# Seven-product K pairs of a two-layer trunk: another order of the products, and one more such pair in each layer's down projection

## The chip, the cores and the metric

The kernel runs on one core of one Trainium2 chip. The metric is the device time of one execution in microseconds (us). Engines are named as in the profile: PE (TensorE) does the matmuls, PEld is its weight load, DVE is VectorE, ACT is ScalarE, POOL is GpSimd, SP is SyncE, which here only starts DMAs. A row such as "L281 DVE TENSOR_TENSOR Tl<-G,Th" is an instruction that line 281 of the kernel issued on DVE and that wrote the tile Tl from the tiles G and Th.

## The reference

Two layers act on 256 tokens of width 2048. Each has a mixer (one input projection, two kinds of attention, an output projection) and a gated feed-forward part of width 5632, each between two RMS norms:

```python
D_MODEL = 2048
SEQ = 256
DEPTH = 2
D_FF = (-(-8 * D_MODEL // 3) + 255) // 256 * 256      # 5632

def swiglu(h, w_gate, w_up, w_down):
    return (jax.nn.silu(h @ w_gate) * (h @ w_up)) @ w_down

def reference(x, w_in, w_o, ..., w_gate, w_up, w_down):
    for l in range(DEPTH):
        h = rms_norm(x, pre_mix_norm[l])
        m = hybrid_mixer(h, l, w_in[l], w_o[l], ...)
        x = x + rms_norm(m, post_mix_norm[l])
        h = rms_norm(x, pre_ffn_norm[l])
        f = swiglu(h, w_gate[l], w_up[l], w_down[l])
        x = x + rms_norm(f, post_ffn_norm[l])
    return x
```

Everything is float32. Nearly all of the work is in the projections `h @ w_in`, `mix @ w_o`, `h @ w_gate`, `h @ w_up` and `... @ w_down`.

## The kernel before

**Weights.** All weights lie in memory in the order in which they are used, cut into pairs of 512 KB. A pair holds two blocks of 128 rows (K) by 512 columns. SP loads them into tiles `raw` (a ring of four). PE multiplies in a rounded float32, so each pair is split: ACT writes the high part `hi` (L307, or L279 in a mixed pair) and DVE the low part `lo` (L317, or L281). `hi` and `lo` are rings of six. A product of tokens and weights is then three matmuls with a moving block of 512 columns: high by high (L1084), high by low (L1085), low by high (L1086).

**Eight and seven.** A K pair (256 rows of K) for two column blocks and two halves of the tokens is a 2 by 2 by 2 block product: eight products, 24 matmuls. Those are `eight` in gate and up (matmuls at L1250) and `down` (L1356, L1357, L1359). For chosen K pairs the kernel uses the Strassen–Winograd form with seven products, 21 matmuls: `seven_products` (L1105), called for the input projection (L1066), the output projection (L1173), gate and up (L1257) and down (L1368). It sums into the four result banks `banks` and into four further banks, `p1`, `p6`, `p7` and `q5`, which `shared_part` (L1122) adds to the results once, after the last seven of a group of columns.

The seven products need sums of tokens and sums of weights. `token_sums` (L1088) makes the four token sums s1 to s4 on DVE (L1091 to L1094) and splits them into `sh` (ACT, L1101) and `sl` (DVE, L1102). `mixed_weights` (L263) makes the weights of five products out of two loaded pairs. The first pair is loaded into `G`. The second is loaded into `T` by SP (L257), and POOL adds a block of the first one to it with an accumulating DMA (L258). Then, in order:

- t1 and b22 are the two halves of the pair split from `T`: `hi` by ACT, `lo` by DVE at L281
- t2 is a difference inside `T` (DVE, L290, 128x512); its parts are `Th` (ACT, L279) and `Tl` (DVE, L281, 128x512)
- `G` plus t2 (DVE, L291, 128x1024) gives t3 and t4; their parts are `Th` (ACT, L279) and `Tl` (DVE, L281, 128x1024)

So t3 is the weight that is ready last but for t4, which comes out of the same operation. `Th` and `Tl` are rings of two. `G` and `T` are rings of three (`T` of four in gate).

**Stages of a layer.** The input projection runs first, then attention, then the output projection (matmuls at L569 to L571 in `unit`), whose result is normalized (`rescale`, L595 to L627, with its square root as a logarithm and an exponential on ACT, L602 and L603) and turned by PE (`transposed`, L485) with the parts read off by ACT (L488) and DVE (L493). Gate and up then run in 11 chunks of 512 columns, eight K pairs each, of which chunk 0 has two sevens, chunk 1 three, chunks 2 and 10 four, and chunks 3 to 9 five:

```python
SEVEN = (2, 4, 5, 6)
MORE_SEVEN = (2, 3, 4, 5, 6)
MORE_AT = (3, 4, 5, 6, 7, 8, 9)
MORE_ORDER = (0, 2, 1, 3, 4, 5, 6, 7)
```

Down runs in two halves of 1024 columns with 22 K pairs each. `DOWN_SEVEN` (L51) lists, for either half, the K pairs that are sevens. Before each K pair, tokens are split into `jh` (ACT, L1332) and `jl` (DVE, L1334), up to two K pairs ahead, in rings of four.

**What sets the order.** The code is written in the order of the products, with weights split four pairs ahead (`LOOKAHEAD`). A scheduler of the language then places the instructions on each engine: they run in program order on an engine in the end, but that order is the scheduler's, which can put a ready instruction ahead of an earlier one. Side chains (attention, transposes of a finished chunk) are advanced by `tick`. So the order in which `seven_products` issues its products also moves instructions of DVE and ACT.

Of the kernel before, what the change touches and what calls it, by code (L numbers as in the profile page):

```python
# [47 lines left out]
MORE_AT = (3, 4, 5, 6, 7, 8, 9)  # L48
MORE_ORDER = (0, 2, 1, 3, 4, 5, 6, 7)
FORM_AT = {(0, 1): 4, (0, 2): 6, (0, 5): 5, (1, 3): 2, (2, 4): 3}  # L50
DOWN_SEVEN = ((4, 7, 10, 12, 15, 17, 20), (3, 5, 8, 10, 13, 15, 18))  # L51

AFTER = mybir.DependencyInfo(mybir.DependencyClass.Sync, mybir.DependencyReason.DATA)

# [26 lines left out]
def weight_order():  # L81
# [3 lines left out]
    def queue_pair(name, l, kp, c):  # L85
        order.append((name, l, kp, c))
        return len(order) - 1
# [3 lines left out]
    for l in range(L):  # L91
# [20 lines left out]
        for half in range(2):  # L112
            for kp in range(FF // P // 2):
                for c in (2 * half, 2 * half + 1):
                    lay["down"][c, kp] = queue_pair("w_down", l, kp, c)
                if kp in DOWN_SEVEN[half]:
                    sevens.add(lay["down"][2 * half + 1, kp])
# [50 lines left out]
def kernel(  # L168
# [30 lines left out]
    def four_banks(odd, names):  # L199
        makers = (bank, bank, bank, last_bank) if odd else (acc_bank,) * 4  # L200
        return [make(n) for make, n in zip(makers, names)]
# [143 lines left out]
    def weights(i, ahead):  # L345
        feed(i + 1 + ahead)
        return ready[i]
# [198 lines left out]
    def tick():  # L546
        clock[0] += 1
        for e in list(running):
            if e[0] <= clock[0]:
                try:  # L550
                    n = next(e[1])
                    e[0] = clock[0] + (PACE if n is None else n)
                except StopIteration:
                    running.remove(e)
# [508 lines left out]
    def seven_in(banks, extra, sums, xT, l, cc, kp, first, last):  # L1063
        hi, lo = weights(plan[l]["in"][cc[0], kp], LOOKAHEAD)
        m = weights(plan[l]["in"][cc[1], kp], LOOKAHEAD)
        seven_products(banks, extra, sums, *pair_blocks(xT, kp), hi, lo, m, first, last)  # L1066
# [14 lines left out]
    def product(a, stat, moving, first, last):  # L1081
        sh, sl = stat
        hi, lo = moving
        nc.tensor.matmul(a, sh, hi, start=first, stop=False, skip_group_check=open_sums[0])  # L1084
        nc.tensor.matmul(a, sh, lo, start=False, stop=False, skip_group_check=open_sums[0])  # L1085
        return nc.tensor.matmul(a, sl, hi, start=False, stop=last, skip_group_check=open_sums[0])  # L1086
# [18 lines left out]
    def seven_products(banks, extra, sums, a11, a12, a22, hi, lo, m, first, last):  # L1105
        s1, s2, s3, s4 = sums
        p1, p6, p7, q5 = extra
        todo = (
            (p1, a11, (hi[:, 0, :], lo[:, 0, :]), first, last),
            (banks[0], a12, (hi[:, 1, :], lo[:, 1, :]), False, False),  # L1110
            (q5, s1, m["t1"], first, last),
            (p7, s3, m["t3"], first, last),
            (p6, s2, m["t2"], first, last),
            (banks[1], s4, m["b22"], False, False),
            (banks[2], a22, m["t4"], False, False),
        )
        for n, job in enumerate(todo):
            if n % 2 == 0:
                tick()
            newest_seven[0] = product(*job)  # L1120
# [14 lines left out]
    for l in range(L):  # L1135
# [27 lines left out]
        for kp in LATE_O:  # L1163
            i, j = (plan[l]["o"][c, kp] for c in (2, 3))
            if kp not in O_SEVEN:
                for c, i in ((2, i), (3, j)):
                    unit({t: accs[c, t] for t in range(NT)}, mix, i, kp, range(NT), kp == LATE_O[0], False)
                continue
            if kp == O_SEVEN[0]:
                extra = four_banks(False, [f"{q}_o{l}" for q in ("p1", "p6", "p7", "q5")])  # L1170
            hi, lo = weights(i, LOOKAHEAD)
            m = weights(j, LOOKAHEAD)
            seven_products(got, extra, forms[kp], *pair_blocks(mix, kp), hi, lo, m, kp == O_SEVEN[0], kp == O_SEVEN[-1])  # L1173
            if kp == O_SEVEN[-1]:
                for t in range(NT):
                    mg[t, 1] = pool.tile([P, 2, CW], F32, tag="qk", bufs=4, name=f"mg_o{l}_{t}_1")
                shared_part(extra, [mg[t, 1][:, h, :] for t in range(NT) for h in range(2)])
                for c in (2, 3):
                    nc.vector.tensor_tensor(out=accs[c, 1], in0=accs[c, 1], in1=mg[1, 1][:, c - 2, :], op=shared_sign(1, c - 2))
# [72 lines left out]
        def seven(banks, extra, c, kp, first, last):  # L1252
            hi, lo = weights(plan[l]["gate"][c, kp], LOOKAHEAD)
            m = weights(plan[l]["up"][c, kp], LOOKAHEAD)
            e, o = xT[2 * kp], xT[2 * kp + 1]
            a11, a12, a22 = (e[:, 0, 0:P], e[:, 1, 0:P]), (o[:, 0, 0:P], o[:, 1, 0:P]), (o[:, 0, P:S], o[:, 1, P:S])
            seven_products(banks, extra, forms[kp], a11, a12, a22, hi, lo, m, first, last)  # L1257

        for c in range(FF // CW):
            banks = four_banks(1 - c % 2, [f"c{q}_{l}_{c}" for q in ("11", "12", "21", "22")])  # L1260
# [62 lines left out]
        for half in range(2):  # L1323
            split, forms = {}, {}
            mine = DOWN_SEVEN[half]

# [71 lines left out]
            for t in range(NT):  # L1398
# [4 lines left out]
                for c in cc:  # L1403
                    for kp in range(nkp - tail, nkp):
# [4 lines left out]
                        for kk in range(2):  # L1409
                            sh, sl = jh[:, kk, t * P : (t + 1) * P], jl[:, kk, t * P : (t + 1) * P]  # L1410
                            last = kp == nkp - 1 and kk == 1
# [63 lines left out]
```

## Time and profile before

Three runs took 2187.52 to 2189.52 us.

| what | before |
|---|---|
| median of the runs | 2189.1 us |
| the profiled execution, its own time | 2188.99 us |
| its span, first to last instruction | 2187.3 us |
| granted clock of TensorE | 0.999 |
| busy DVE, ACT, POOL | 88%, 64%, 11% of the span |
| DMA queues of SP: bytes, share of the 16 engines | 436 MB, 57.7% |
| DMA queue of POOL | 32.6 MB, 8.9% |

The span is the profiled execution without what lies before its first and after its last instruction. Busy time of PE counts pipelined matmuls with modelled ends; a row's duration is longer than the step from one matmul to the next. Rows of a group read: line, engine, operation, output<-inputs, shapes, count, then busy us and mean ns of one, then the idle time of the engine just before them and what ended it. Rows of a timeline read: start, duration, engine, line, operation, with idle before and its releaser in brackets. Rows of waits read: who waited for whom, us in total, times, longest.

### The profile page before, as it was taken

The page shows a single profiled execution, that of the slowest core. Times are in us where ns is not written, and L with a number is a line of the kernel's source. Part 1 is how long each engine was busy: PE and PEld are TensorE (multiplying, and loading weights), DVE is VectorE, ACT ScalarE, POOL GpSimd, SP SyncE. Part 2 cuts the span into 40 slices and gives each one's busy share as a digit, 9 for nine tenths or more (in the row PEclk, how much of TensorE's full clock was granted, in tenths as well). Part 3 has the DMA queues.
Part 4 walks back from the last instruction along what each step waited for, and adds up shares of the span by engine and source line. Part 5 has one row for each costly group of instructions (what it writes and reads, how often), then busy time and mean ns, then how long its engine had stood idle before and what let it go on. Part 6 is the DMA issues. An engine that isn't in the chain of part 4 may idle for free.

```text
span 2187.3 us, 28757 instructions
## 1 busy us (share of the span) xinstructions
PE 2170.0 (99%) x9950; PEld 1782.2 (81%) x9950; DVE 1914.1 (88%) x2639; ACT 1393.4 (64%) x2083; POOL 251.1 (11%) x241
## 2 busy tenths in 40 slices
PE   9999999999999999999999999999999999999998
PEld 7888888788888888888878888887888888888886
DVE  7888658999999999989878886589999999999997
ACT  7666665766666656666665656657566666666664
POOL 2100000031221220000010000001212212200000
PEclk9999999999999999999999999999999999999999
DMA  9545554587887876767465555555878877767683
GB/s 324 194 163 174 192 189 168 184 291 234 243 261 222 234 228 228 231 216 255 146 241 174 181 176 182 193 170 184 292 226 255 249 222 231 239 216 233 207 265 101
DMA packets 140563, 470.96 MB, mean 215 GB/s; under 512 B 15984, under 2 KB 17008, under 8 KB 139904
## 3 DMA queue, kind: packets, MB, share of 16 engines
q1 hardware_dynamic: 121952, 436.03, 57.7%
q0 software_dynamic: 17888, 32.55, 8.9%
q8 instruction: 78, 1.28, 0.2%
q10 hardware_dynamic: 576, 0.54, 0.1%
q14 instruction: 69, 0.57, 0.1%
HBM read 460.67 MB, written 8.39 MB: 214 GB/s over the span
## 4 chain that ended last, share of the span: by engine, by line
PE 87%; DVE 7%; issue 2%; DMA 2%; ACT 1%; SPq 0%; DVEq 0%; ACTq 0%
PE c L1250 16%; PE in L1084 7%; PE in L1086 7%; PE in L1085 7%; PE dn L1356 4%; PE dn L1357 4%; PE dn L1359 4%; PE p L1085 2%; PE c L1086 2%; PE c L1084 2%; PE c L1085 2%; PE p L1086 2%; PE p L1084 2%; PE o L569 2%; PE o L570 2%
## 5 line engine op out<-in xcount | busy, mean ns | idle before, releaser
L317 DVE TENSOR_TENSOR lo<-raw,hi 128x1024 fp32r<-128x1024 f32 x472 | 567.8, 1221 | 99.0 <-ACT hi L307 97.9
L307 ACT ACTIVATE hi<-raw 128x1024 fp32r<-128x1024 f32 x494 | 509.8, 1055 | 144.2 <-PE c L1086 36.8
L1250 PE MATMUL c<-hi,xF 128*128 128x512 f32 x1280 | 346.0, 391 | 0.1
L1250 PEld LDWEIGHTS c<-hi,xF 128*128 128x128 f32 x1280 | 238.3, 188 | 49.1 <-DVE xF L493 0.6
L258 POOL DMA_DIRECT2D T<-in_weights_in_turn_dram x124 | 108.8, 877 | 1343.6 <-DMA T<-in_weights_in_turn_dram 764.8
L1250 PE MATMUL c<-lo,xF 128*128 128x512 f32 x640 | 198.2, 390 | 2.5 <-DVE lo L317 2.5
L1356 PE MATMUL dn<-hi,jh 128*128 128x512 f32 x432 | 168.2, 389 | 0.0
L1357 PE MATMUL dn<-lo,jh 128*128 128x512 f32 x432 | 168.1, 389 | 0.0
L307 ACT ACTIVATE hi<-G 128x1024 fp32r<-128x1024 f32 x124 | 131.1, 1057 | 52.1 <-DMA G<-in_weights_in_turn_dram 20.8
L281 DVE TENSOR_TENSOR Tl<-G,Th 128x1024 fp32r<-128x1024 f32 x124 | 151.2, 1220 | 14.5 <-ACT Th L279 14.5
L279 ACT ACTIVATE hi<-T 128x1024 fp32r<-128x1024 f32 x124 | 130.3, 1051 | 51.0 <-PE c L1086 29.8
L279 ACT ACTIVATE Th<-G 128x1024 fp32r<-128x1024 f32 x124 | 130.8, 1055 | 47.8 <-DVE G L291 47.5
L281 DVE TENSOR_TENSOR lo<-T,hi 128x1024 fp32r<-128x1024 f32 x124 | 156.5, 1262 | 2.9 <-ACT hi L279 2.4
L291 DVE TENSOR_TENSOR G<-G,T 128x1024 f32<-128x1024 f32 x124 | 151.2, 1219 | 2.1
L1250 PEld LDWEIGHTS c<-lo,xF 128*128 128x128 f32 x640 | 120.1, 188 | 28.2 <-DVE lo L317 3.0
L317 DVE TENSOR_TENSOR lo<-G,hi 128x1024 fp32r<-128x1024 f32 x106 | 129.2, 1219 | 12.2 <-ACT hi L307 12.0
L1359 PE MATMUL dn<-hi,jl 128*128 128x512 f32 x432 | 133.0, 389 | 0.0
L1084 PE MATMUL in<-hi,xT 128*128 128x512 f32 x328 | 131.4, 402 | 0.5 <-ACT hi L889 0.5
L279 ACT ACTIVATE Th<-T 128x512 fp32r<-128x512 f32 x124 | 78.2, 631 | 83.6 <-DVE T L290 82.9
L1084 PE MATMUL in<-hi,xI 128*128 128x512 f32 x328 | 131.1, 401 | 0.0
L1085 PE MATMUL in<-lo,xI 128*128 128x512 f32 x328 | 128.0, 390 | 0.3 <-DVE lo L317 0.3
L1086 PE MATMUL in<-hi,xI 128*128 128x512 f32 x328 | 127.9, 391 | 0.0
(485 smaller groups left out, 4917.7 us busy)
## 6 DMA issues: line engine op xcount, KB each, us to landing
raw<-in_weights_in_turn_dram SPq DMA_DIRECT2D x494, 512.0 KB, 4.6
T<-in_weights_in_turn_dram SPq DMA_DIRECT2D x124, 512.0 KB, 5.5
G<-in_weights_in_turn_dram SPq DMA_DIRECT2D x124, 512.0 KB, 5.6
T<-in_weights_in_turn_dram POOLq DMA_DIRECT2D x124, 256.0 KB, 5.7
GU<-in_weights_in_turn_dram SPq DMA_DIRECT2D x32, 512.0 KB, 6.2
V<-in_weights_in_turn_dram SPq DMA_DIRECT2D x8, 512.0 KB, 3.9
away_ffn<-x SPq DMA_DIRECT2D x8, 512.0 KB, 7.4
xd<-away_ffn SPq DMA_DIRECT2D x8, 512.0 KB, 9.5
```

The costliest lines, as they stand in the source:

```text
L279: nc.scalar.activation(h, w, AF.Copy)
L281: newest_rest[i] = nc.vector.tensor_tensor(out=l, in0=w, in1=h.bitcast(F32), op=ALU.subtract)
L291: nc.vector.tensor_tensor(out=g, in0=g, in1=t2.unsqueeze(1).to_broadcast([P, 2, CW]), op=ALU.add)
L307: nc.scalar.activation(hi, raw, AF.Copy)
L317: rest = nc.vector.tensor_tensor(out=lo, in0=raw, in1=hi.bitcast(F32), op=ALU.subtract)
L1084: nc.tensor.matmul(a, sh, hi, start=first, stop=False, skip_group_check=open_sums[0])
L1085: nc.tensor.matmul(a, sh, lo, start=False, stop=False, skip_group_check=open_sums[0])
L1086: return nc.tensor.matmul(a, sl, hi, start=False, stop=last, skip_group_check=open_sums[0])
L1250: nc.tensor.matmul(a, stat[part], w[j][:, kk, :], start=first and kk + n == 0, stop=last and kk == 1 and n == 2)
L1356: nc.tensor.matmul(accs[c, t], sh, hi[:, kk, :], start=first, stop=False, skip_group_check=open_sums[0])
L1357: nc.tensor.matmul(accs[c, t], sh, lo[:, kk, :], start=False, stop=False, skip_group_check=open_sums[0])
L1359: nc.tensor.matmul(accs[c, t], sl, hi[:, kk, :], start=False, stop=last, skip_group_check=open_sums[0])
```

## The change

`seven_products` issues the product with b22 fourth instead of sixth, and the products with t2 and t3 behind it, t2 first. And the first half of down in either layer has eight sevens instead of seven: up to K pair 12 they are the same, behind it every second K pair is one.

```diff
-DOWN_SEVEN = ((4, 7, 10, 12, 15, 17, 20), (3, 5, 8, 10, 13, 15, 18))
+DOWN_SEVEN = ((4, 7, 10, 12, 14, 16, 18, 20), (3, 5, 8, 10, 13, 15, 18))
...
         todo = (
             (p1, a11, (hi[:, 0, :], lo[:, 0, :]), first, last),
             (banks[0], a12, (hi[:, 1, :], lo[:, 1, :]), False, False),
             (q5, s1, m["t1"], first, last),
+            (banks[1], s4, m["b22"], False, False),
+            (p6, s2, m["t2"], first, last),
             (p7, s3, m["t3"], first, last),
-            (p6, s2, m["t2"], first, last),
-            (banks[1], s4, m["b22"], False, False),
             (banks[2], a22, m["t4"], False, False),
         )
```

The same products are summed into the same banks. In the order of instructions of the two builds PE has 6 matmuls fewer, DVE 18 operations more (nine in each layer: what a seven needs beyond an eight), ACT six more and POOL two more accumulating loads.

## The prediction

> **What bounds the kernel now.** I read the page first: busy shares, then the chain that ended last.
>
> ```profile
> PE 2170.0 (99%) x9950; PEld 1782.2 (81%) x9950; DVE 1914.1 (88%) x2639; ACT 1393.4 (64%) x2083; POOL 251.1 (11%) x241
> PE 87%; DVE 7%; issue 2%; DMA 2%; ACT 1%; SPq 0%; DVEq 0%; ACTq 0%
> ```
>
> TensorE (PE) sets the end. Its busy share says little about what remains, because the modelled ends of pipelined matmuls overlap. Start times tell more. This is the timeline of PE in the second half of down, the first matmul of one seven and the first behind it:
>
> ```profile
> 1001.13 0.39 PE L1084 MATMUL p_d<-hi,jh 128*128 128x512 f32 x1
> ...
> 1005.89 0.39 PE L1356 MATMUL dn<-hi,jh 128*128 128x512 f32 x1
> ```
>
> 21 matmuls take 4.76 us: a matmul is worth 0.2268 us, not the 0.39 of its row. A wait therefore loses 0.39 − 0.23 = 0.16 us before the profile calls it idle. So two views are read together, the waits of PE and its groups by stage. The waits:
>
> ```profile
> PE p L1085 <- DVE Tl L281: 3.5, 8, 0.7
> PE c L1250 <- DVE lo L317: 2.5, 2, 1.2
> PE p L1084 <- ACT Th L279: 0.3, 1, 0.3
> ```
>
> The longest sum is for Tl, the low parts of t2 and t3, which the vector engine (DVE) makes. The groups that read Tl and Th, by stretch of the span: the input projection; chunks 0 to 2 of layer 0, then of layer 1; chunks 3 to 8 of layer 0, then of layer 1; and two groups of chunk 9 of layer 0.
>
> ```profile
> L1085 PE MATMUL p_in<-Tl,shin 128*128 128x512 f32 x16 | 6.3, 396 | 0.0
> ...
> L1085 PE MATMUL p<-Tl,sh 128*128 128x512 f32 x18 | 7.3, 408 | 0.1
> ...
> L1085 PE MATMUL p<-Tl,sh 128*128 128x512 f32 x18 | 7.3, 408 | 0.6 <-DVE Tl L281 0.6
> ...
> L1085 PE MATMUL p<-Tl,sh 128*128 128x512 f32 x48 | 19.3, 403 | 0.7 <-DVE Tl L281 0.6
> ...
> L1085 PE MATMUL p<-Tl,sh 128*128 128x512 f32 x48 | 19.4, 403 | 1.7 <-DVE Tl L281 1.7
> ...
> L1085 PE MATMUL p<-Tl,sh 128*128 128x512 f32 x8 | 3.2, 404 | 0.7 <-DVE Tl L281 0.7
> L1084 PE MATMUL p<-Th,sh 128*128 128x512 f32 x8 | 2.9, 403 | 0.3 <-ACT Th L279 0.3
> ```
>
> A stall costs its idle time, 0.16 us ahead of it, and a restart that shows as a mean above the 390 ns of an undisturbed row. Chunks 3 to 8 of layer 1, one stall in each: 1.7 + 6 × 0.16 + 48 × 0.013 = 3.3 us; of layer 0: 0.7 + 0.96 + 0.62 = 2.3. Chunk 9: (0.7 + 0.16 + 0.11) + (0.3 + 0.16 + 0.10) = 1.5. From start to start, with 0.227 taken off, the timeline gives in sum: input projection 0.26, chunks 0 to 2 0.95 and 1.48 (some of it at Th), chunks 3 to 8 2.06 and 3.28, chunk 9 1.60. Together **9.6 us**: all that a reorder of these products can win.
>
> One of them, chunk 4 of layer 0, in the timelines of ACT, DVE and PE:
>
> ```profile
> 592.21 1.06 ACT L307 ACTIVATE hi<-raw 128x1024 fp32r<-128x1024 f32 x1 [1.03 <-PE c L1086]
> ...
> 593.85 1.22 DVE L317 TENSOR_TENSOR lo<-raw,hi 128x1024 fp32r<-128x1024 f32 x1
> 594.98 1.22 DVE L281 TENSOR_TENSOR Tl<-G,Th 128x1024 fp32r<-128x1024 f32 x1
> ...
> 595.87 0.39 PE L1085 MATMUL c<-lo,sh 128*128 128x512 f32 x1
> 596.26 0.50 PE L1085 MATMUL p<-Tl,sh 128*128 128x512 f32 x1
> 596.59 0.40 PE L1086 MATMUL p<-Th,sl 128*128 128x512 f32 x1
> ...
> 603.44 0.62 PE L1250 MATMUL c<-lo,xF 128*128 128x512 f32 x2
> ```
>
> The step to 596.26 is 0.39 and the next 0.33: 0.27 us lost. The reader is to see why: DVE put the low part of a raw pair (593.85) ahead of the Tl of K pair 5, though PE reads that raw pair only at 603.44, in K pair 7. And ACT began its high parts late, because it waited for a PE product to free a slot of the ring "hi".
>
> **The change part by part.** *Count.* One more seven per layer has 21 matmuls where an eight had 24: 2 × 3 × 0.2268 = **−1.36 us**, if PE isn't starved there. The Trainium skill, page "TensorE: Matmul & The Clock Gate", section "Back-to-back issue gap", gives about 131 ns a matmul at 512 columns for a sustained stream, by which this term would be an estimated 0.79 us; the row above contradicts it with 227 ns, and the measurement decides.
>
> *Order, in gate and up.* What decides is the order on each engine in the two builds. In chunks 3 to 9 DVE now runs the Tl of K pair 5 one 128x1024 operation earlier, 1.14 us by the step from 593.85 to 594.98; for K pair 6 it is two. PE reaches t3 one matmul (0.23) later. The mean loss there is 5.34 / 12 = 0.45 us a chunk, the relief 1.37, so they go: −2.06 − 3.28. The displaced low part ends 1.14 later, at 596.2 instead of 595.07, and is read at 603.44, so nothing is late next. In chunk 1 t3 comes 3 matmuls later (0.68): of 0.41 and 0.94 go 0.41 and 0.68. In chunk 2 (0.71 in both layers) DVE is 1.14 earlier: all goes. The input projection's t3 moves 6 matmuls: −0.26. Chunk 0 keeps its order and its 0.37. Chunk 9 of layer 0 waits for Th first, behind a late load; 1.14 + 0.23 covers 1.35 of 1.60. b22 is multiplied two products sooner, so "hi" comes free 6 × 0.227 = 1.36 us sooner and ACT starts sooner; I count nothing more for it. Sum of the order: **−8.75 us**. Bounds: nothing, and 9.63.
>
> DVE pays for it in its own time only if it has some:
>
> ```profile
> 500.00:700.00 200.00, 199.64 (x896) 164.00 (x895) 193.75 (x218) 129.80 (x151) 45.25 (x34) 1.00 0.81 242
> ```
>
> In this window (columns: PE, PEld, DVE, ACT, POOL busy, then clock, DMA share, GB/s) DVE idles 6.25 of 200 us, 1.3 us per chunk of about 41, against 0.34 (layer 0) and 0.55 (layer 1) by which a chunk is to shorten. The granted clock is 1.00.
>
> *Between the output projection and gate.* Here the order on PE moves against the change. DVE and PE:
>
> ```profile
> 390.63 2.74 DVE L627 SCALAR_TENSOR_TENSOR x<-mg_o,tot_o,x 128x512 f32<-128x512 f32 x4
> ...
> 399.63 0.22 DVE L476 SCALAR_TENSOR_TENSOR tot_o<-tot_o 128x1 f32<-128x1 f32 x1 [0.42 <-ACT tot_o L603]
> ...
> 403.33 1.21 DVE L317 TENSOR_TENSOR lo<-raw,hi 128x1024 fp32r<-128x1024 f32 x1
> ...
> 391.43 0.66 PE L485 MATMUL xT_ps<-ident,x 128*128 128x128 f32 x4
> ...
> 404.60 0.50 PE L1250 MATMUL c<-lo,xF 128*128 128x512 f32 x1 [1.25 <-DVE lo L317]
> ```
>
> The transposes at 391.43 start as soon as x is there. In the new order four matmuls stand ahead of them. PE had lost about 0.25 us waiting for x, which those fill, so the transposes come 0.62 to 0.7 later. ACT works back to back from there to L603, DVE waits 0.42 for that, and PE 1.25 for DVE's low part: nothing on this path has slack. **+0.62 us** a layer, **+1.24** in all; bounds 0 (were ACT to catch up) and 2 × 4 × 0.227 = 1.8.
>
> *Down, first half.* K pairs 10 to 20 now alternate seven and eight: 45 matmuls, 10.2 us. DVE before, around K pairs 10 and 12, and PE's use of K pair 12's Tl:
>
> ```profile
> 907.58 1.23 DVE L281 TENSOR_TENSOR Tl<-G,Th 128x1024 fp32r<-128x1024 f32 x1 [0.52 <-ACT Th L279]
> ...
> 913.20 0.69 DVE L1334 TENSOR_TENSOR jl<-act,jh 128x512 fp32r<-128x512 f32 x1 [1.53 <-ACT jh L1332]
> 914.15 1.22 DVE L317 TENSOR_TENSOR lo<-G,hi 128x1024 fp32r<-128x1024 f32 x1 [0.26 <-ACT hi L307]
> ...
> 918.77 1.22 DVE L291 TENSOR_TENSOR G<-G,T 128x1024 f32<-128x1024 f32 x1
> 919.91 0.68 DVE L281 TENSOR_TENSOR Tl<-T,Th 128x512 fp32r<-128x512 f32 x1
> 920.51 1.22 DVE L317 TENSOR_TENSOR lo<-raw,hi 128x1024 fp32r<-128x1024 f32 x1
> 921.65 1.21 DVE L281 TENSOR_TENSOR Tl<-G,Th 128x1024 fp32r<-128x1024 f32 x1
> ...
> 925.20 0.39 PE L1085 MATMUL p_d<-Tl,sh 128*128 128x512 f32 x1
> ```
>
> From start to start a 128x1024 operation is worth 1.14 and a 128x512 one 0.60 us. Seven and eight need six and five of them (the token sums L1091 to L1094 run before K pair 10): 6.84 + 3.0 = 9.9 us, 0.3 below PE's period. The Tl ends at 922.8, 2.34 us ahead of its use; t3 six matmuls later makes 3.7. I take 0, since nothing is late. Its cost if the waits of 0.52, 1.53 and 0.26 stayed in every period is a rival. The extra accumulating load of POOL adds 256 KB a layer:
>
> ```profile
> T<-in_weights_in_turn_dram SPq DMA_DIRECT2D x124, 512.0 KB, 5.5
> ...
> T<-in_weights_in_turn_dram POOLq DMA_DIRECT2D x124, 256.0 KB, 5.7
> ```
>
> Load and accumulate need 11.2 us one behind the other; with three slots of T and 10.2 us between sevens some 25 us lie between a slot's release and its next use. Nothing.
>
> Sum against the profiled execution's 2188.99 us (0.1 below the median): 2189.0 − 1.36 − 8.75 + 1.24 = **2180.1 us**.
>
> **The rivals.** *DVE sets the pace of gate.* It is 97% busy in the window above, so chunks 3 to 8 would lose the same time at another tile. For it: stalls differ from chunk to chunk under one order, as where a queue runs at its limit. Against it: 1.3 us idle a chunk. It keeps 3.41 of the 8.75: 2189.0 − 1.36 − 3.41 + 1.24 = 2185.5.
>
> *It doesn't do what it says.* A scheduler already places instructions, and in chunks 3 to 8 PE's order moves by one matmul only. If DVE's earlier Tl then waits for Th, made no sooner on ACT, just the count and the projection remain: 2189.0 − 1.36 − 0.26 + 1.24 = 2188.6. Against it: Th of K pair 5 stands behind hi on ACT, which the earlier b22 frees.
>
> *Slower: DVE falls behind in down.* With the three waits in every period DVE needs 9.9 + 2.3 = 12.2 us, with two restarts of 0.11 a deficit of 2.2 against 10.2; five periods make 11.0, less the 2.34 of slack 8.7 a layer, 17.3 in all: 2197.4. It decides from a DVE period of 11.5 us on (4.4 a layer, which eats the gain). Against it: the 1.53 is for jh, freed by PE, so a DVE that is late doesn't meet it; and one jl now stands between Th's input and Tl, over the 0.52.
>
> **How the numbers follow.** Forecast 0.63, DVE's pace 0.17, no effect 0.07, slower in down 0.13. This measurement tells 0.2% (4.4 us) from no change. The forecast lies beyond that; of DVE's pace 0.05 does too, and of the slow case 0.03 is too small to count. Faster 0.68, same 0.12 + 0.07 + 0.03 = 0.22, slower 0.10. The low end takes all stalls and no loss (2189.0 − 9.6 − 1.4 = 2178.0) and 1.2 for the spread of the runs; the high end takes in DVE's pace with 2.0 more. The forecast's own range is 2176.8 to 2184.
>
> **What would show it.** Right: the group p from Tl has a mean near 391 ns and under 1 us idle, chunks shorten by 0.3 to 0.6 us, PE's wait at L1250 comes 0.6 us later behind the same wait, and down's first half is 0.68 us shorter with no PE wait. Wrong: new PE waits for lo or Tl between K pairs 12 and 20 of down, a bank wait at the chunk ends, or Tl stalls as before.

## The result and the profile after

The changed kernel takes 2182.1 us, the median of nine runs (2180.45 to 2184.95), against 2188.9 of the kernel before (nine runs, 2187.29 to 2190.99): a ratio of 0.997 with a 95% interval of 0.9961 to 0.9979, so 4.6 to 8.5 us were gained, 6.8 in the medians. The forecast was 2180.1, a gain of 8.9 us.

The page of the changed kernel, busy shares and the chain that ended last:

```profile
PE 2166.0 (99%) x9944; PEld 1781.7 (82%) x9944; DVE 1920.7 (88%) x2657; ACT 1400.4 (64%) x2089; POOL 260.5 (12%) x243
PE 94%; DVE 3%; ACT 2%; issue 1%; DMA 0%; SPq 0%; DVEq 0%; ACTq 0%
```

PE's share of the chain rose from 87% to 94%, DVE's fell from 7% to 3%. PE's longest waits (who for whom, us in total, times, longest):

```profile
PE c L1250 <- DVE lo L317: 2.5, 2, 1.3
...
PE c L1250 <- DVE xF L493: 1.5, 2, 0.7
...
PE pT_df L823 <- DVE w L1127: 0.5, 2, 0.2
```

The wait for Tl, 3.5 us before, is gone from the list; the waits for xF and w are new. The groups that read Tl, for the same stretches as before (input projection; chunks 0 to 2 of layer 0 and of layer 1; chunks 3 to 8 of layer 0 and of layer 1; chunk 9 of layer 0):

```profile
L1085 PE MATMUL p_in<-Tl,shin 128*128 128x512 f32 x16 | 6.2, 389 | 0.0
...
L1085 PE MATMUL p<-Tl,sh 128*128 128x512 f32 x18 | 7.1, 395 | 0.0
...
L1085 PE MATMUL p<-Tl,sh 128*128 128x512 f32 x18 | 7.2, 401 | 0.0
...
L1085 PE MATMUL p<-Tl,sh 128*128 128x512 f32 x48 | 19.0, 396 | 0.0
...
L1085 PE MATMUL p<-Tl,sh 128*128 128x512 f32 x48 | 18.9, 393 | 0.0
...
L1085 PE MATMUL p<-Tl,sh 128*128 128x512 f32 x8 | 3.2, 404 | 0.0
```

No row has idle time left, and the means stand at 389 to 404 ns instead of 396 to 408. Chunk 4 of layer 0 shows the new order, DVE first, then PE:

```profile
595.18 1.23 DVE L281 TENSOR_TENSOR Tl<-G,Th 128x1024 fp32r<-128x1024 f32 x1
...
598.06 1.22 DVE L317 TENSOR_TENSOR lo<-raw,hi 128x1024 fp32r<-128x1024 f32 x1
...
594.10 0.39 PE L1084 MATMUL q<-hi,sh 128*128 128x512 f32 x1
...
596.14 0.39 PE L1084 MATMUL p<-Th,sh 128*128 128x512 f32 x1
596.46 0.50 PE L1085 MATMUL p<-Tl,sh 128*128 128x512 f32 x1
596.79 0.40 PE L1086 MATMUL p<-Th,sl 128*128 128x512 f32 x1
```

The Tl of K pair 5 (595.18) now stands ahead of the low part of the raw pair. In this execution it was still 0.09 us late, with the restart 0.2.

The same tile's high part Th, made by ACT, says more. Here it is in that chunk, before and then changed:

```profile
593.18 1.04 ACT L279 ACTIVATE Th<-G 128x1024 fp32r<-128x1024 f32 x1
```

```profile
594.09 1.06 ACT L279 ACTIVATE Th<-G 128x1024 fp32r<-128x1024 f32 x1 [0.62 <-DVE G L291]
```

Before, Th was there at 594.22, and Tl started 0.76 us later, behind the raw pair's low part; in chunks 3 to 9 of both layers it was 0.5 to 1.2 us. In the changed kernel Tl starts 0.03 us behind its Th in all fourteen of these chunks. PE gains less than that shift, because Th itself now ends at varying times. From the first matmul of q5 in that seven (594.10 here, 594.05 before) to the end of Tl the mean of the fourteen was 2.37 us before, 1.92 in the changed kernel and 1.43 in a second execution of it. In chunk 4 of layer 0 it was 2.15 and 2.30, so this chunk shows the order and not the gain.

Down's first half, from its first matmul to that of the second half, before and then changed:

```profile
858.77 0.39 PE L1356 MATMUL dn<-hi,jh 128*128 128x512 f32 x1
...
974.61 0.39 PE L1356 MATMUL dn<-hi,jh 128*128 128x512 f32 x1
```

```profile
857.40 0.39 PE L1356 MATMUL dn<-hi,jh 128*128 128x512 f32 x1
...
972.55 0.39 PE L1356 MATMUL dn<-hi,jh 128*128 128x512 f32 x1
```

115.84 and 115.15 us: 0.69 less, three matmuls. In the same way, as differences of such start times in PE's timeline, this table takes the execution apart for most of the kernels below (us, one profiled execution each). Layer 0's chunk 10 has no row: it took 41.70 or 41.71 us in each of them.

| stretch | before | changed | changed again | order alone | down alone | old order in o | t3 before b22 | t3 before t2 | old in o and in |
|---|---|---|---|---|---|---|---|---|---|
| start, first columns of in | 89.56 | 89.82 | 89.05 | 89.93 | 89.66 | 89.08 | 90.59 | 90.57 | 89.89 |
| rest of in, attention | 202.24 | 202.53 | 202.57 | 202.52 | 202.22 | 202.52 | 202.53 | 202.53 | 202.21 |
| output projection to gate | 96.82 | 97.77 | 97.71 | 97.70 | 96.85 | 96.79 | 97.74 | 97.72 | 96.79 |
| gate, chunks 0 to 2 | 131.02 | 130.12 | 130.13 | 130.23 | 131.02 | 130.14 | 131.05 | 130.58 | 130.15 |
| chunks 3 to 9 | 291.23 | 289.16 | 287.56 | 288.06 | 289.46 | 288.11 | 290.18 | 288.56 | 288.22 |
| down, first half | 115.84 | 115.15 | 115.15 | 115.83 | 115.15 | 115.16 | 115.15 | 115.15 | 115.15 |
| second half to layer 1's gate | 508.63 | 509.84 | 509.96 | 510.02 | 508.61 | 509.02 | 509.85 | 509.94 | 508.69 |
| layer 1, chunks 0 to 2 | 131.51 | 130.21 | 130.45 | 130.27 | 131.40 | 130.62 | 131.55 | 131.00 | 130.36 |
| layer 1, chunks 3 to 9 | 290.88 | 288.12 | 287.20 | 287.20 | 290.05 | 288.05 | 289.53 | 287.29 | 287.20 |
| layer 1, chunk 10 and down | 272.91 | 272.26 | 272.26 | 272.90 | 272.23 | 272.23 | 272.22 | 272.23 | 272.22 |

Down's rows and those up to gate repeat within 0.1 us wherever their order is the same, the one up to layer 1's gate within 0.2. The first row and chunks 3 to 9 vary between executions. A part of the first row's spread is the pace of the first matmuls: with t3 before t2 nine steps from 6.39 to 10.32 us are longer than 0.227, most of them 0.43, 1.9 us in sum, and in the changed kernel again only one is. 287.20 us (41.03 a chunk) is seven chunks without a wait.

### The profile page after: what moved, and what is told of

The parts are those of the page before. It is cut to its first block, busy times and chain, and to the rows that moved or that the text cites. A ratio compares the mean times of both kernels' runs of the same rounds, so it can differ in the third digit from the quotient of the medians.

```text
span 2181.7 us, 28784 instructions
## 1 busy us (share of the span) xinstructions
PE 2166.0 (99%) x9944; PEld 1781.7 (82%) x9944; DVE 1920.7 (88%) x2657; ACT 1400.4 (64%) x2089; POOL 260.5 (12%) x243
## 4 chain that ended last, share of the span: by engine, by line
PE 94%; DVE 3%; ACT 2%; issue 1%; DMA 0%; SPq 0%; DVEq 0%; ACTq 0%
PE c L1250 19%; PE in L1084 7%; PE in L1086 7%; PE in L1085 7%; PE dn L1357 4%; PE dn L1356 4%; PE dn L1359 4%; PE p L1085 3%; PE c L1084 3%; PE p L1084 3%; PE p L1086 3%; PE c L1085 3%; PE c L1086 3%; PE o L569 2%; PE o L571 2%; PE o L570 2%
## 5 line engine op out<-in xcount | busy, mean ns | idle before, releaser
L317 DVE TENSOR_TENSOR lo<-raw,hi 128x1024 fp32r<-128x1024 f32 x468 | 561.9, 1220 | 103.3 <-ACT hi L307 102.3
L307 ACT ACTIVATE hi<-raw 128x1024 fp32r<-128x1024 f32 x490 | 501.5, 1053 | 102.3 <-DMA raw<-in_weights_in_turn_dram 41.8
L281 DVE TENSOR_TENSOR Tl<-G,Th 128x1024 fp32r<-128x1024 f32 x126 | 153.9, 1221 | 10.1 <-ACT Th L279 10.1
L1356 PE MATMUL dn<-hi,jh 128*128 128x512 f32 x416 | 162.0, 389 | 0.0
L1357 PE MATMUL dn<-lo,jh 128*128 128x512 f32 x416 | 161.8, 389 | 0.0
L307 ACT ACTIVATE hi<-G 128x1024 fp32r<-128x1024 f32 x126 | 132.9, 1055 | 44.6 <-DMA G<-in_weights_in_turn_dram 27.8
L281 DVE TENSOR_TENSOR lo<-T,hi 128x1024 fp32r<-128x1024 f32 x126 | 159.6, 1266 | 0.3 <-ACT hi L279 0.2
L1084 PE MATMUL in<-hi,xI 128*128 128x512 f32 x328 | 131.1, 401 | 0.0
L1085 PE MATMUL in<-lo,xT 128*128 128x512 f32 x328 | 127.8, 391 | 0.4 <-DVE lo L891 0.4
L1359 PE MATMUL dn<-hi,jl 128*128 128x512 f32 x416 | 128.0, 389 | 0.0
```

Source lines behind the costliest of these rows:

```text
L281: newest_rest[i] = nc.vector.tensor_tensor(out=l, in0=w, in1=h.bitcast(F32), op=ALU.subtract)
L307: nc.scalar.activation(hi, raw, AF.Copy)
L317: rest = nc.vector.tensor_tensor(out=lo, in0=raw, in1=hi.bitcast(F32), op=ALU.subtract)
L1356: nc.tensor.matmul(accs[c, t], sh, hi[:, kk, :], start=first, stop=False, skip_group_check=open_sums[0])
L1357: nc.tensor.matmul(accs[c, t], sh, lo[:, kk, :], start=False, stop=False, skip_group_check=open_sums[0])
L1359: nc.tensor.matmul(accs[c, t], sl, hi[:, kk, :], start=False, stop=last, skip_group_check=open_sums[0])
```

## The experiments

In the diffs, `turn` is the order in which the seven products of the changed kernel's list are issued; the order of the kernel before is `turn=(0, 1, 2, 5, 4, 3, 6)`. The runs were taken in three sets after the first one, each with the kernel before beside it (2187.4, 2187.3 and 2187.2 us), and the ratios are to that one.

**The two parts alone.** The changed kernel with the old `DOWN_SEVEN`, and the kernel before with the new one.

```diff
-DOWN_SEVEN = ((4, 7, 10, 12, 14, 16, 18, 20), (3, 5, 8, 10, 13, 15, 18))
+DOWN_SEVEN = ((4, 7, 10, 12, 15, 17, 20), (3, 5, 8, 10, 13, 15, 18))
```

> The new order of the products with the old list of sevens in down. If the two parts simply add, this lacks only the six matmuls: 6 x 0.2268 = 1.36 us slower than the changed kernel, about 5.5 us (0.25%) faster than the kernel before, and its trace shows the same ledger as the changed kernel up to the start of down. Rival: the denser sevens in down cost something hidden later (second half of down, next layer's start); then this one is as fast as the changed kernel or faster.

> The old order of the products with the eighth seven in down. Count theory: 1.36 us faster than the kernel before (ratio 0.9994), 0.68 us in each layer's first half of down, no wait of PE there, all stalls of gate as before (9.6 us of waits for Tl and Th). Rival, DVE falls behind: t3 is read fourth here, 2.34 us behind its making in the trace of before and 1.36 us earlier than in the new order, so PE waits for Tl at K pairs 16 to 20 and the gain shrinks or turns into a loss of up to 8 us a layer.

Measured: the order alone 0.9977 (0.9968 to 0.9985), median 2182.1; down alone 0.9994 (0.9985 to 1.0003), 2186.0 against 2187.4. The runs can't tell the latter from no change, but its traces can: both halves that the eighth seven touches are 0.68 and 0.69 us shorter and the rows up to gate are those of the kernel before within 0.1 us. In the window 858 to 1000 PE has no wait at all, in the old order too. So DVE doesn't fall behind in down, and t3's 2.34 us were enough. Within the noise the parts add.

**The output projection in the old order.**

```diff
-            seven_products(got, extra, forms[kp], *pair_blocks(mix, kp), hi, lo, m, kp == O_SEVEN[0], kp == O_SEVEN[-1])
+            seven_products(got, extra, forms[kp], *pair_blocks(mix, kp), hi, lo, m, kp == O_SEVEN[0], kp == O_SEVEN[-1], turn=(0, 1, 2, 5, 4, 3, 6))
```

> The changed kernel, with the old order kept in the output projection alone. Theory: there the new order puts the seven's products ahead of four matmuls whose end frees a slot of the ring hi, so ACT and the whole chain behind it start 4 x 0.227 = 0.91 us later in each layer; the old order takes that back: 1.8 us faster than the changed kernel, gate's first product 0.9 us earlier in each layer. Forecast's own size of this step: 0.62 a layer, 1.24 in all. Rival: the chain is late for another reason (the shift at the start of the execution, or the attention); then gate's first product stands where it does in the changed kernel.

Measured: 2179.9 us, 0.9963 (0.9951 to 0.9976). That interval overlaps the changed kernel's, so the gain is read from the traces: the stretch to gate fell from 97.77 to 96.79, that of layer 1 from 509.84 to 509.02, 1.8 us in sum. ACT in the kernel before, the changed one and this one:

```profile
381.43 1.06 ACT L307 ACTIVATE hi<-raw 128x1024 fp32r<-128x1024 f32 x1 [3.87 <-PE o L571]
```

```profile
383.00 1.06 ACT L307 ACTIVATE hi<-raw 128x1024 fp32r<-128x1024 f32 x1 [5.10 <-PE o L571]
```

```profile
381.54 1.06 ACT L307 ACTIVATE hi<-raw 128x1024 fp32r<-128x1024 f32 x1 [3.63 <-DVE lo L317]
```

Of the 1.57 us between the first two, 0.66 lie ahead of the output projection, whose first matmul starts at 297.99 and 298.65; 0.91, four matmuls, belong to it. The chain behind it keeps that distance up to the transposes. Here is PE in the changed kernel:

```profile
393.04 1.32 PE L485 MATMUL xT_ps<-ident,x 128*128 128x128 f32 x8
...
396.42 1.19 PE L1250 MATMUL c<-hi,xF 128*128 128x512 f32 x4 [0.74 <-DVE xF L493]
```

**Which part of the new order works.** In gate alone, t3 after t2 but both ahead of b22; then b22 ahead of both, but t3 before t2.

```diff
-            seven_products(banks, extra, forms[kp], a11, a12, a22, hi, lo, m, first, last)
+            seven_products(banks, extra, forms[kp], a11, a12, a22, hi, lo, m, first, last, turn=(0, 1, 2, 4, 5, 3, 6))
...
+            seven_products(banks, extra, forms[kp], a11, a12, a22, hi, lo, m, first, last, turn=(0, 1, 2, 3, 5, 4, 6))
```

> The changed kernel with gate's order q5, t2, t3, b22: t2 and t3 exchanged, b22 left behind them. In the order of instructions DVE again puts the raw pair's low part of K pair 7 ahead of the Tl of K pair 5, as in the kernel before, and PE's product with t3 stands where it stood. Theory (DVE's place of Tl is what matters): the stalls of chunks 3 to 8 come back, 0.3 to 0.8 us in each, chunks of 41.3 to 41.9 us, some 5 us slower than the changed kernel. Rival (t2 ahead of t3 is what matters): chunks of 41.0 to 41.3 us as in the changed kernel, the same time.

> The changed kernel with gate's order q5, b22, t3, t2: only b22 is moved ahead, t3 still before t2. DVE's order is that of the changed kernel; t3 is read 0.68 us earlier. Theory (DVE's place of Tl): relief 1.14 - 0.45 = 0.7 us against the kernel before instead of 1.37, so most stalls go and 0 to 0.4 us a chunk stay where the loss was 0.6 to 0.85: 0.5 to 2.5 us slower than the changed kernel. Rival (t2 ahead of t3 matters): as slow as the kernel before in chunks 3 to 8.

Measured: the first is no faster than the kernel before, 1.0004 (0.9996 to 1.0013). It has six matmuls fewer, but also the new order in the projections, which by the table costs 2.4 us in the rows up to the two gates, less 0.3 in the first columns; its chunks 0 to 9 take 842.3 us in both layers together, against 841.9 with down alone and 844.6 before. The second took 0.9978 (0.9969 to 0.9987), as the changed kernel. DVE and PE of the first one, chunk 4:

```profile
596.40 1.22 DVE L317 TENSOR_TENSOR lo<-raw,hi 128x1024 fp32r<-128x1024 f32 x1
597.54 1.22 DVE L281 TENSOR_TENSOR Tl<-G,Th 128x1024 fp32r<-128x1024 f32 x1
...
597.91 0.39 PE L1085 MATMUL c<-lo,sh 128*128 128x512 f32 x1
598.81 0.50 PE L1085 MATMUL p<-Tl,sh 128*128 128x512 f32 x1 [0.51 <-DVE Tl L281]
```

It is the picture of the kernel before, in all fourteen chunks 3 to 9: the raw pair ahead of Tl, and PE waiting in most of them. With t3 before t2 DVE has the changed kernel's order in all fourteen, and loses 1.5 us there, within the 0.4 to 2.9 of the changed kernel's two executions, although PE reads t3 sooner. So neither the exchange of t2 and t3 nor t3's later place does it in chunks 3 to 9, but b22's place, with which the scheduler puts Tl first on DVE. The same place frees slots of "hi" sooner: in chunks 3 to 8 of layer 0 ACT waited 15.7 us at L307 for PE's products at L1086 before, and not at all in the changed kernel. No run moves one of the two without the other; that DVE's order is needed is read from the traces, where Tl stood 0.5 to 1.2 us behind a finished Th.

In chunks 0 to 2 t3's place counts too (131.05, 130.58 and 130.12 us in layer 0), as forecast for chunk 1. The second kernel was expected 0.5 to 2.5 us slower than the changed one. The runs don't resolve that; by its trace it loses 0.5 and 0.8 us in chunks 0 to 2, and nothing against the means of the changed order in chunks 3 to 9, where it was expected.

**q5 behind b22.** In its profile the changed kernel waits some 0.3 us for q5's bank in chunks 5, 7 and 9.

```diff
-            seven_products(banks, extra, forms[kp], a11, a12, a22, hi, lo, m, first, last)
+            seven_products(banks, extra, forms[kp], a11, a12, a22, hi, lo, m, first, last, turn=(0, 1, 3, 2, 4, 5, 6))
```

> The changed kernel, in gate and up with the q5 product behind the b22 product, three matmuls (0.68 us) later. In the changed kernel PE waits 0.3 us for the bank of q5 in chunks 5, 7 and 9, and 0.2 us for Tl in chunks 4, 6 and 8 of layer 0. Theory of a local wait: the waits for q5's bank go, 5 x 0.3 = 1.5 us faster. Rival, DVE's pace: chunks take 41.3 us because DVE, with its waits for ACT, needs 41.3 us a chunk; then the loss moves to the waits for Tl of the same or the next chunk, chunks 4 to 8 of layer 0 stay at 41.2 to 41.4 us each, and the time stays within 0.4 us.

Measured: 2182.0 us, 0.9973 (0.9962 to 0.9984), no difference to the changed kernel that the runs resolve. The waits for q5 are gone, and two waits for Tl took their place in layer 0 (chunk 6 took 41.54 us, chunk 9 42.07, with 0.72 us idle at Tl). In layer 1 the chunks took 41.02 to 41.08. So the wait for a bank was one more place at which DVE's lateness shows. It isn't a fixed pace of 41.3 us: layer 1 has none.

**More help from POOL, and a fourth slot for G.** Two tries to free DVE: one more low part in a chunk on POOL; G in four slots, T in three.

```diff
-            for n in (1, 2):
+            for n in (1, 2, 7):
                 helped[lay["gate"][c, gate_order(c)[n]]] = n == 1
```

```diff
-... ("G", 3, [P, 2, CW]), ("T", 4, [P, 2, CW])):
+... ("G", 4, [P, 2, CW]), ("T", 3, [P, 2, CW])):
...
-        mix_raw[:] = gu, 3, 4, plan[l]["down"][0, 0]
+        mix_raw[:] = gu, 4, 3, plan[l]["down"][0, 0]
```

> The changed kernel, with one more low part in each of chunks 1 to 10 on POOL instead of DVE (the gate pair of the last K pair; 20 operations of 1.14 us less on DVE, each 2.6 to 3.2 us on POOL and read some 8 us after it was made). PE's order of instructions is the same. Theory, DVE's pace bounds the chunks that still lose time (41.2 to 41.4 instead of 41.02): with 1.14 us less work DVE is ahead, all chunks 3 to 9 fall to 41.02 to 41.05, 1.5 to 3 us faster than the changed kernel. Rival, single late tiles (a load, a Th of ACT) set these waits: the chunks stay spread between 41.0 and 41.4, no gain. Second rival: POOL's work slows DVE's by sharing its memory access, and the accumulating loads queue behind it on POOL; then chunks are longer than 41.4.

> The changed kernel with four slots for G and three for T in gate, instead of three and four. PE, DVE and ACT run the same instructions in the same order; only loads move. In every chunk ACT waits about 2 us for the G of K pair 4, whose load SP issues only when DVE has read the Tl's of a G three sevens before, and DVE then waits 0.4 to 0.9 us for ACT. Theory (that late load is what the chunks that lose time lose it to): with the fourth slot the wait of ACT goes, chunks 3 to 9 take 41.02 to 41.05 us in both layers, 1 to 2 us faster than the changed kernel. Rival: T, which needs a load and an accumulating load one behind the other, becomes the late one with three slots; chunks get longer, by up to some us each.

Measured: 1.0316 (1.0302 to 1.033) and 1.0174 (1.016 to 1.0188), both far slower, each as its rival that named another resource had it. With POOL's help chunk 3 of layer 0 took 52.7 us and chunks 4 to 8 42.8 to 44.6. The timeline of DVE and POOL in it, and then a wait of DVE:

```profile
565.06 3.37 DVE L281 TENSOR_TENSOR Tl<-T,Th 128x512 fp32r<-128x512 f32 x1
568.36 0.68 DVE L290 TENSOR_TENSOR T<-T 128x512 f32<-128x512 f32 x1
...
565.13 2.74 POOL L310 TENSOR_TENSOR lo<-raw,hi 128x1024 fp32r<-128x1024 f32 x1
```

```profile
DVE G L291 <- POOL lo L310: 32.6, 5, 10.5
```

A DVE operation that otherwise takes 0.68 us ends only 0.56 us behind the POOL operation beside it, and DVE also waits for a low part that POOL makes behind its accumulating load. The kernel ties the first of its two low parts on POOL to the end of a seven (`add_manual_dep`, with the reason "the shared port"); the added one isn't tied, and no run tried that. With four slots for G, ACT in layer 0's chunks 3 to 8, changed kernel and then this one:

```profile
ACT hi L307 <- DMA G<-in_weights_in_turn_dram: 13.2, 6, 2.4
```

```profile
ACT hi L279 <- DMA T<-in_weights_in_turn_dram: 25.9, 5, 5.5
```

The six waits for G are gone, and waits for T, twice as long in sum, stand there. So neither kernel could show whether the late load of G is what chunks 3 to 9 lose their time to.

**The same kernel again, and three that keep the old order where it cost.** The changed kernel itself; the same with the old `turn` in the input projection alone; with the old `turn` in the output and the input projection; and the latter with q5 behind b22 in gate. The edits are those shown above, at the calls of these projections and of gate.

> The changed kernel as it is, for a comparison on one chip with the three that follow. Its profile lost 0.2 to 0.35 us in each of chunks 4 to 8 of layer 0; others with the same order in gate lost it in other chunks. Theory (these losses depend on when loads land, not on the order): another execution loses a different amount in different chunks, between 0 and 2 us in gate. Rival (they are fixed by the order): the same chunks, the same losses within 0.1 us.

> The changed kernel with the old order in the input projection alone. In the changed kernel PE waits 0.16 us, with its restart 0.27, for DVE's w (L1127) ahead of a transpose of the attention, once in each layer, and has lost the 0.26 us stall of layer 0's first sevens. Theory: both come back as they were, the stretch up to the output projection 0.29 us shorter and the first one 0.30 us longer in layer 0, 0.27 shorter in layer 1: 0.26 us in sum. Rival: the wait at the transpose is chance; then it stays.

> The changed kernel with the old order in the output and the input projection; gate, up and down keep the new one. The two gains seen alone should add: 1.8 us (output projection) and 0.2 to 0.3 (input projection), 2.0 us faster than the changed kernel, some 8.5 to 9 us faster than the kernel before, near what was forecast. Rival: the earlier start of gate only meets later waits (DVE and loads are no earlier), then less than 1 us remains.

> As the one before, and q5 behind b22 in gate. If the waits for q5's bank are losses of their own, up to 0.9 us faster than the one before; if they only stand where DVE's lag shows first, no difference beyond 0.5 us.

Measured on one chip in one set, against 2187.2 of the kernel before: changed again 2180.7, 0.9971 (0.996 to 0.9981); old order in both projections 2179.3, 0.9963 (0.9951 to 0.9976); with q5 behind b22 the same, 2179.3, 0.9964 (0.9951 to 0.9976). Old order in the input projection alone took 2181.0 in one run of another set, too few for a verdict. Its first stretch was 0.28 us longer (45.42 instead of 45.14 from the second to the third pair of column groups), attention 202.21 instead of 202.53, the stretch to layer 1's gate 509.65 instead of 509.84. The wait for w is gone from its trace and from that of the kernel with both projections in the old order, and stands in those of the changed kernel, both times, and of the one with the old order in the output projection alone: it goes with the order. The two projections' gains add in the traces: 97.71 − 96.79 and 509.96 − 508.69 and 202.57 − 202.21 make 2.55 us, less 0.28, 2.3; the medians differ by 1.4. The execution of the changed kernel again, chunks 3 to 8 of layer 0 and of layer 1:

```profile
L1085 PE MATMUL p<-Tl,sh 128*128 128x512 f32 x48 | 18.7, 389 | 0.0
...
L1085 PE MATMUL p<-Tl,sh 128*128 128x512 f32 x48 | 18.7, 389 | 0.0
```

Not one stall at Tl, where the first execution of the same kernel had five in these chunks; one wait of 0.25 us for q5's bank is left, in chunk 5 of layer 0. Chunks 3 to 9 took 287.56 and 287.20 us instead of 289.16 and 288.12. So what is lost there differs between executions of one kernel. With q5 behind b22 and the old order in both projections no chunk from 3 to 9 lost anything in the profiled execution (287.20 us in either layer), and the median was still the same 2179.3.

## Why the prediction was right, and where its sizes were off

*Count.* Forecast −1.36. Down's two first halves are 0.69 us shorter each in the profiles, and 0.68 or 0.69 without the new order. Right.

*Order in gate and up.* Forecast −8.49 (and 0.26 in the input projection); the mechanism is shown by the pair of orders above. In the first pair of profiles chunks 0 to 9 gained 0.90 + 2.07 and 1.30 + 2.76, 7.0 us; by the second profile of the changed kernel 9.3. Two steps were mis-sized. One is "together 9.6 us": it took the stalls of one execution for those of the kernel. The kernel with down alone has gate's old order, and lost 2.6 us less in chunks 3 to 9 (289.46 and 290.05 against 291.23 and 290.88). Chunk 9 of layer 0, forecast with 1.35, is such a case: 42.69 us in the kernel before, 41.67 with down alone. The other is the relief of 1.14 us, taken as one whole operation of DVE. In the chunk shown Th was there only at 594.22, so a Tl put first would have been 0.76 us earlier and not 1.14; and the mean of the fourteen chunks, measured against PE, moved by 0.45 us in the first profile and 0.94 in the second. So the changed order still lost 1.4 us in chunks 3 to 9 of both layers, in the mean of five profiles, where the forecast left 0.25. The rival "it doesn't do what it says" had the link right that the forecast left out, for Tl now follows directly behind Th; but Th comes early enough for most of the stalls to go.

*Between the output projection and gate.* Forecast +1.24, measured 0.95 in layer 0 and 1.21 in layer 1's stretch, of which the wait for w is 0.2 to 0.4: some 1.8 to 2.0 for both. The step said that four matmuls fill PE's 0.25 us wait for x. They don't: x is late by all four as well, because the seven's products stand ahead of the matmul at L571 whose end frees a slot of "hi" for ACT. Undoing the order there gave 1.8 us back in the traces.

*The input projection.* −0.26 was forecast, −0.30 came (the first stretch of the input projection, 45.44 to 45.14). Not foreseen: DVE's `shared_part` there is later, and a transpose of the attention waits for w, 0.29 us in layer 0 (202.24 to 202.53), 0.2 to 0.4 in layer 1. The forecast read PE's order there and not DVE's behind it.

*Down, first half.* Forecast at 0 beside the count, and so it is. The slower rival is refuted by the window without a wait.

*DVE's pace.* It got a chance of 0.17 and a time of 2185.5. The changed kernel's first profile seemed to bear it out, with 41.2 to 41.4 us in chunks 4 to 8 of layer 0 and, in five chunks, a wait for a bank, which the forecast had named among the signs against itself. Layer 1 of the second profile, with the same order and seven chunks in 287.20 us, refutes a fixed pace. What is shown is that DVE has little reserve and that the two executions of the changed kernel lost 2.9 and 0.4 us in chunks 3 to 9 of both layers; which event starts it stays open. That it is a late load was argued from the waits of ACT for G and wasn't shown. Another candidate is POOL: in the changed kernel again a low part on DVE beside one on POOL took 1.73 us instead of 1.22, in chunk 4 of layer 0, ahead of the wait in chunk 5. It isn't the only one: with the order alone no such operation of DVE was long, and chunk 9 of layer 0 still lost 0.41 us.

*The sum.* Chunks 3 to 9 take 290.3 and 290.2 us in the mean of the three profiles with the old order on DVE (before, down alone, t3 before b22) and 288.2 and 287.6 in that of the five with the changed kernel's gate in the table (changed, changed again, order alone, and the two with the old order in o): −4.7. Chunks 0 to 2 add −0.9 and −1.1, the count −1.3 (0.69, and 0.65 up to the end of the last row), the first stretch of the input projection −0.3, and +0.29, +0.95 and +1.21 go against it: −5.9 us, where the medians of two sets of runs gave −6.8 and −6.6. The 3.0 us between this and the forecast's −8.9 are the order in gate and up (1.8) and the stretches around the attention and the output projection (1.2). Both erred to the same side, so nothing cancelled.

## What to carry to other kernels

The order in which products are issued also decides what the engine that makes their operands does first, through the scheduler; compare the orders on every engine, and when a product moves, look at each tile whose release it delays, not only at the operands that it waits for. Stalls of an engine with little reserve differ between executions, so a gain worked out from one trace needs a second execution of the same kernel, or a margin as large as that difference. An order that pays in one stage can cost in another: keep it where it pays (old in both projections, new in gate: 2179.3 us, 8.0 less than the kernel before and 1.4 less than the changed one in the medians of one set).

## What the runs showed of the hardware

In the kernel with more help from POOL, twenty 128x512 operations of DVE (L281 and L290, all their tiles in SBUF) took 2.76 to 3.37 us instead of 0.68, each beside one operation of 2.7 to 3.1 us on POOL, and each ended 0.54 to 0.56 us behind it. Operations of DVE with an operand in PSUM beside POOL's kept their time: L1303 and L1307 took 0.68 and 0.69. The Trainium skill, page "SBUF — State Buffer", section "Who interferes with whom", says that a DVE instruction with two inputs in SBUF contends with a GpSimd instruction that reads SBUF, and that this contention is an exclusive lock; the trace agrees, with these numbers.
